# A hybrid decoder layer on one core: the sampled tokens' state space steps moved into tiles of their own, later, with a gate and a norm of their own, and the prompt's gate sums moved further behind their rows

## The chip, the cores and the metric

One core of a Trainium2 chip runs the whole kernel in one launch. The metric is the time of an execution on the device in microseconds (us); the figure for a kernel is the median of several runs. Engines are named as in the profile: PE (TensorE) does matmuls, DVE (VectorE), ACT (ScalarE) and POOL (GpSimd) do the elementwise work, SP issues transfers (DMA).

## The reference

One layer of a decoder on 1024 new prompt positions and 8 sampled tokens (one step each, with a past). Cut to what matters:

```
h = rmsnorm(x, norm1_w);  proj = h @ w_in          # columns: q, f, i, g, z, xBC, dt
o_a = HGRN2(q, f, i) ; o_a = rmsnorm(o_a) * silu(g)             # 8 heads of 128
xBC = silu(conv4(xBC));  X, B, C = split(xBC);  dt = softplus(dt + bias)
y = ssd_scan(X*dt, A*dt, B, C, S0) + D*X                        # 16 heads of 64, 2 groups
y = rmsnorm_per_group(y * silu(z)) * ssm_norm_w
x = x + concat(o_a, y) @ w_out
x = x + (silu(conv3(gate)) * val) @ w_down ;  out = rmsnorm(x)
```

For a sampled token `ssd_scan` is one step: new state S = exp(A dt) S0 + B (dt X), y = C S + D X. The prompt's 1024 positions are done in 8 chunks of 128. The kernel returns outputs and all the new states.

## The kernel before, in words

Activations lie with channels on the 128 partitions and tokens along the columns: NT = 1032 columns, the 1024 (T) of the prompt and behind them 8 (ND) of the sampled tokens. An input projection job (`in_job`, L290) makes 128 output channels: for each of 3 column chunks of 344 it issues 24 matmuls into one of three PSUM banks (`psmm`) and hands the bank to an eviction. 72 matmul steps make a job.

The order of PE's instructions is written by hand (`manual_schedule`, L1119). A list of jobs gives the backbone: x0 to x3, the B and C jobs and x4 to x7 (the conv'd channels of both state space groups), z0 to z3, the first head's f0, q0, v0, sg0, then z4 to z7, f1 and so on to head 7, then the output mix. `drive` (L266) steps through the jobs and puts the parts of another stream between their matmuls: the chunk steps of group 0 (`ssd(0)`, L713) run beside the jobs up to x7, those of group 1 from there up to v0, and each `head` in its turn. `after(n, work)` (L229) calls work n matmul steps later; what it issues on PE stands at that place. On the other engines a scheduler sets the order, and each engine keeps its queue.

A chunk step has two parts. `ssd_front` (L530) makes the decay matrix (csb: fetch, ACT Relu L541 and Exp L542, DVE L557), B C products (bg, bt), and transposed, scaled X (xp, xdt L554). `ssd_back` (L560) does the matmuls yo (with the state S), st and yd, the state update S (DVE L580) and the writing back into X's tile (L593).

The sampled tokens: `ssm_decode(g, i)` (L625) does one 128-channel tile. Twice, for 4 tokens each, it fetches Bb, Cb and the state Sd, scales Sd by the decay (4 ACT instructions, L638), multiplies Bb (DVE L639), adds (L640), stores the new state, multiplies by Cb (POOL L642) and reduces (DVE L643). Its result goes into columns 1024 to 1031 of the X tile. It is called at the beginning of jobs x5, x7, z0, z1 (group 0) and z4 to z7 (group 1).

`ssm_gate` (L653): each z job's eviction applies Silu (ACT L670), multiplies X's tile (DVE L671) and adds the squares to `gacc`. For the last z job of a group each chunk's sum goes to `rstd` (L681) 36 steps later in group 0, 50 in group 1: a matmul `ms` with ones sums over partitions, and `rstd_of` (L646) makes 1/sqrt on 344 columns (one ACT instruction from another function table and three DVE steps). After the last chunk `tail` (L690) scales the four X tiles of the group (DVE L694) and writes them to `mix_d` in DRAM, from where the output mix reads them after the heads.

Tiles come from pools (L42): "big" has 10 buffers of 1056 columns, so a head's q, v, sg and k wait for what lay there, X tiles among them. Matmul banks beside psmm's three: 4 "mx", 1 "nx" (ms, the head's vd and others).

A head's input (`head_in`, L806) evicts f, q, v and sg with Sigmoid, Silu, Copy and Silu (L818); f's end scales f (ACT L811) and makes k (DVE L812).

Of the kernel before, what the change touches and what calls it, by code (L numbers as in the profile page):

```python
# [8 lines left out]
F32 = mybir.dt.float32  # L9
F32R = mybir.dt.float32r  # L10
U8 = mybir.dt.uint8
AF = mybir.ActivationFunctionType
ALU = mybir.AluOpType
# [3 lines left out]
P = 128  # L17
DM = 1024
T = 1024
ND = 8  # L20
NT = T + ND
CH = 344
NCH = 3
# [27 lines left out]
def hybrid_layer(  # L51
# [9 lines left out]
    V, A, G, PE, SP = nc.vector, nc.scalar, nc.gpsimd, nc.tensor, nc.sync  # L61
# [9 lines left out]
    def nm(s):  # L71
        cnt[0] += 1
        return f"{s}_{cnt[0]}"
# [4 lines left out]
    const = part.enter_context(tc.tile_pool(name="const", bufs=1, side="right"))  # L78
    small = part.enter_context(tc.tile_pool(name="small", bufs=2, side="right"))
    tmp = part.enter_context(tc.tile_pool(name="tmp", bufs=1, side="right"))  # L80

    def tl(tag, name, dt=F32):
        w, n = TAGS[tag]
        return (work if tag in ("hT", "big", "e", "g") else tmp).tile([P, w], dt, tag=tag, bufs=n, name=nm(name))
# [4 lines left out]
    def bank(s, tag="mx"):  # L89
        return psmx.tile([P, 512], F32, tag=tag, bufs=NBANK[tag], name=nm(s))  # L90

    def mm(out, lhsT, rhs, start=True, stop=True):
        PE.matmul(out, lhsT, rhs, start=start, stop=stop)  # L93
# [55 lines left out]
    def col(name, i=0):  # L149
        c = vlay[name] + i  # L150
        return vcol[:, c:c + 1]
# [58 lines left out]
    chunks = [slice(c * CH, (c + 1) * CH) for c in range(NCH)]  # L210
# [18 lines left out]
    def after(n, work):  # L229

        later.append([n, work])
# [106 lines left out]
    Xg = [[None] * 4 for _ in range(2)]  # L338
    BT, CT, S = [None, None], [None, None], [None, None]
    last11 = const.tile([P, XT, 11], F32, name="last11")  # L340
    mix_d = dram.tile([16, P, NT], F32, name="mix_d")
    bc_d = dram.tile([4, ND, P], F32, name="bc_d")

    def conv_tail(acc, ext, nw, wname, bname, j, ntile, n):
        A.activation(acc[:, :n], ext[:, :n], AF.Identity, bias=col(bname, j), scale=col(wname, j))
        for q in range(1, nw):
            V.scalar_tensor_tensor(acc[:, :n], ext[:, q:q + n], col(wname, q * ntile + j), acc[:, :n],
                                   op0=ALU.mult, op1=ALU.add)

    def xbc_open():  # L350
        ext = tl("e", "ext")
        G.memset(ext[:, 0:3], 0.0)
        return ext

    def xbc_evict(j, ext, c, cs, ps):
        e = min(cs.stop, T)
        A.copy(ext[:, 3 + cs.start:3 + e], ps[:, :e - cs.start])
        if c == 2:
            V.tensor_copy(ext[:, 3 + T:3 + T + 32].rearrange("p (b r) -> p b r", r=4)[:, :, 3:4],
                          ps[:, T - cs.start:].unsqueeze(2))  # L360
            V.tensor_copy(last11[:, j, :], ps[:, CH - 11:])

    def xbc_close(j, ext):
        G.tensor_copy(ext[:, 3 + T:3 + T + 32].rearrange("p (b r) -> p b r", r=4)[:, :, 0:3],
                      bufT[:, j, :].rearrange("p (b r) -> p b r", r=3))
        n = T + 32
        acc = tl("big", "xbc")
        conv_tail(acc, ext, 4, "cw", "cb", j, XT, n)
        A.activation(acc[:, :T], acc[:, :T], AF.Silu)
        A.activation(acc[:, T:NT], acc[:, T + 3:T + 32:4], AF.Silu)  # L370
        return acc

    def xbc_job(j, put):
        ext = []
        def begin():
            ext.append(xbc_open())
            if j in (5, 7):
                ssm_decode(0, (5, 7).index(j))

        in_job(f"x{j}", OFF_X + j * P, lambda c, cs, ps: xbc_evict(j, ext[0], c, cs, ps), begin=begin, end=lambda: put(xbc_close(j, ext[0])))  # L380

# [20 lines left out]
    ones = keep.tile([P, P], F32, name="ones")  # L402
# [24 lines left out]
    for c, cs in enumerate(chunks):  # L427
        ps = psmm.tile([P, 512], F32, tag="mm", name=nm("dt"))
# [9 lines left out]
    for i in range(9):  # L438
        n = P if i < 8 else ND
# [171 lines left out]
    def d4(t):  # L611
        return t.rearrange("p (b n) -> p b n", n=P)
# [12 lines left out]
    def ssm_decode(g, i):  # L625
        j = g * 4 + i
        xdd = small.tile([P, 2, ND], F32, tag="xdd", name=nm("xdd"))
        xdec = Xg[g][i][:, T:NT]
        V.tensor_tensor(xdd[:, 0, :], xdec, ddb[:, 0, j, :], op=ALU.mult)
        for b0 in (0, 4):  # L630
            bs = slice(b0, b0 + 4)
            Bb, Cb = tl("d", "Bb")[:, :512], tl("d", "Cb")[:, :512]
            for t_, r in ((Bb, 2 * g), (Cb, 2 * g + 1)):
                fetch(t_, bc_d[r, bs].rearrange("b n -> (b n)").unsqueeze(0).to_broadcast([P, 512]))
            Sd = tl("ld", "Sd")
            fetch(d4(Sd), state_ssm[0, bs, 2 * j:2 * j + 2].rearrange("b h p n -> (h p) b n"))
            for b in range(4):
                A.activation(d4(Sd)[:, b, :], d4(Sd)[:, b, :], AF.Copy, scale=ddb[:, 1, j, b0 + b:b0 + b + 1])  # L638
            V.tensor_tensor(d4(Bb), d4(Bb), cb(xdd[:, 0, bs]), op=ALU.mult)  # L639
            V.tensor_tensor(Sd, Sd, Bb, op=ALU.add)  # L640
            SP.dma_start(ssm_sample[0, bs, 2 * j:2 * j + 2].rearrange("b h p n -> (h p) b n"), d4(Sd))
            G.tensor_tensor(Cb, Sd, Cb, op=ALU.mult)  # L642
            V.tensor_reduce(xdd[:, 1, bs], d4(Cb), axis=mybir.AxisListType.X, op=ALU.add)  # L643
        V.scalar_tensor_tensor(xdec, xdec, d_bc[:, j:j + 1], xdd[:, 1, :], op0=ALU.mult, op1=ALU.add)

    def rstd_of(dst, tmp, ps, n):  # L646

        A.activation(dst, ps, AF.Abs_reciprocal_sqrt, bias=epsc, scale=1.0 / n)
        V.scalar_tensor_tensor(tmp, ps, n * EPS, dst, op0=ALU.add, op1=ALU.mult)
        V.scalar_tensor_tensor(tmp, tmp, -0.5 / n, dst, op0=ALU.mult, op1=ALU.mult)  # L650
        V.scalar_tensor_tensor(dst, tmp, 1.5, dst, op0=ALU.add, op1=ALU.mult)

    def ssm_gate(g):  # L653
        acc = []

        def z_job(i):
            j = g * 4 + i

            def begin():
                if i == 0:  # L660
                    acc.append(tl("g", "gacc"))
                if g:
                    ssm_decode(1, i)
                elif i < 2:
                    ssm_decode(0, i + 2)

            def evict(c, cs, ps):
                Y = Xg[g][i][:, cs]
                sz = tl("z", "sz")[:, :CH]
                A.activation(sz, ps, AF.Silu)  # L670
                V.tensor_tensor(Y, Y, sz, op=ALU.mult)  # L671
                if i == 0:
                    A.activation(acc[0][:, cs], Y, AF.Square)
                else:
                    A.activation(sz, Y, AF.Square)
                    (V if g or i == 3 else G).tensor_tensor(acc[0][:, cs], acc[0][:, cs], sz, op=ALU.add)
                if i == 3:
                    after(36 + 14 * g, lambda: rstd(c))
            in_job(f"z{j}", OFF_Z + j * P, evict, begin=begin)

        def rstd(c):  # L681
            cs = chunks[c]
            ps = bank("ms", "nx")
            mm(ps[:, :CH], ones, acc[0][:, cs])
            rstd_of(acc[0][:, cs], tl("z", "nt")[:, :CH], ps[:, :CH], 512)

            if c == NCH - 1:
                tail()

        def tail():  # L690
            for i in range(4):
                j = g * 4 + i
                Y = Xg[g][i][:, :NT]
                V.scalar_tensor_tensor(Y, Y, col("sn", j), acc[0][:, :NT], op0=ALU.mult, op1=ALU.mult)  # L694
                SP.dma_start(mix_d[8 + j], Y)

        for i in range(4):
            z_job(i)
# [107 lines left out]
    def head_in(h):  # L806
        t = {}

        def f_end():
            f, k = t["f"], tl("big", "k")  # L810
            A.activation(f[:, :NT], f[:, :NT], AF.Identity, bias=lbt[:, 0, h:h + 1], scale=lbt[:, 1, h:h + 1])  # L811
            V.tensor_scalar(k[:, :NT], f[:, :NT], -1.0, 1.0, op0=ALU.mult, op1=ALU.add)  # L812
            t["k"] = k

        for n, off, func in (("f", OFF_F, AF.Sigmoid), ("q", OFF_Q, AF.Silu), ("v", OFF_I, AF.Copy),
                             ("sg", OFF_G, AF.Silu)):
            def evict(c, cs, ps, n=n, func=func):
                A.activation(t[n][:, cs], ps, func)  # L818

            def begin(n=n):  # L820
                t[n] = tl("e" if h == 0 and n == "f" else "big", n)

            if h == H - 1 and n == "sg":
                in_job_last(f"{n}{h}", off + h * P, evict, begin)
            else:
                in_job(f"{n}{h}", off + h * P, evict, begin, f_end if n == "f" else None)
        return t
# [539 lines left out]
    with tc.manual_schedule(engines={mybir.EngineType.PE}):  # L1367
# [56 lines left out]
        for r0 in range(0, FT - RND, RND):  # L1424
# [3 lines left out]
            for m in range(0, KT, 2):  # L1428
                wh, wl = wload(w_down[0, rows, m * P:(m + 2) * P], nk, 2 * P)
                for i in range(2):  # L1430
# [3 lines left out]
                    for c, cs in enumerate(quarters):  # L1434
                        ps = down(lambda k: (wh[:, k, :], wl[:, k, :]), nk, slice(i * P, (i + 1) * P), acts, c)
# [14 lines left out]
    for c in (3, 0, 1, 2):  # L1450
        cs = quarters[c]
        for m in range(KT):
            ps = down(lambda k: wd[k], nk, slice(m * P, (m + 1) * P), acts, c)
            V.tensor_tensor(xT[m][:, cs], xT[m][:, cs], ps, op=ALU.add)
        for t0 in range(cs.start, cs.stop, P):
            n = min(P, cs.stop - t0)
# [10 lines left out]
            for i in range(2):  # L1467
# [4 lines left out]
                else:  # L1472
                    V.scalar_tensor_tensor(ot[i][:n], tb[i][:n, :], ss[:n, 3:4], fw[:n, ds],  # L1473
                                           op0=ALU.mult, op1=ALU.mult)
# [31 lines left out]
```

## Time and profile before

| | |
|---|---|
| median of 3 runs | 1764.88 us (1764.72 to 1768.95) |
| the profiled execution | 1763.89 us, its span 1762.2 us |
| mean granted PE clock | 0.994 |
| PE busy in the span | 1713.2 us (97%) |
| DVE, ACT, POOL busy | 1105.4, 812.3, 482.0 us |

The profile is one execution. A line of the list of waits names the waiting engine and instruction, the instruction that released it, the total, the number and the longest of such waits. A line of the stretches gives for a window the busy time and number of instructions of each engine, the granted clock, the DMA share and GB/s. A line of a timeline starts with the start time and the duration; "x4" is four merged instructions, and what stands in brackets is idle time of the engine ahead of it and what ended it. L93 is the line of the helper that issues all matmuls.

### The profile page before, as it was taken

Reading aid. Unit: us, or ns where it says so; the run is one execution under the profiler, and the core shown is the slowest. Engines: PE = TensorE matmul, PEld = TensorE weight load, DVE = VectorE, ACT = ScalarE, POOL = GpSimd, SP = SyncE. Lnnn points to the kernel's source line nnn. Section 1 sums busy time; section 2 is a strip of 40 time slices with the busy share of each in tenths; the row PEclk is TensorE's granted clock in tenths of the full one; section 3 lists DMA queues with packets and bytes.
Section 4 is the critical chain, followed back from the end, with each engine's and each line's share of the span. In section 5 each row is a group of like instructions: output and inputs, shape, how many; then the busy total and the mean of one; then the engine's idle time right before and its main releaser. Section 6 shows DMA issues by size and latency. Waiting matters only on the chain. (4 is left out here: it accounts for less than half of the span.)

```text
span 1762.2 us, 38558 instructions
## 1 busy us (share of the span) xinstructions
PE 1713.2 (97%) x16111; PEld 1662.8 (94%) x16111; DVE 1105.4 (63%) x1988; ACT 812.3 (46%) x1450; POOL 482.0 (27%) x485
## 2 busy tenths in 40 slices
PE   7999899999999999999899999999999999999998
PEld 6999799998999999999799989999999999999997
DVE  6668966575554554466636688776667777445545
ACT  7577698454544454454423374334333434111114
POOL 2103332120110110112220355666666664000002
PEclk9999999999999999999899999999999999999999
DMA  5355744643321332234336742222222226422312
GB/s 166 68 147 155 189 117 136 179 139 105 88 89 51 98 87 80 69 115 143 110 113 212 245 127 73 73 85 85 85 73 73 80 78 217 152 85 78 98 61 97
DMA packets 249828, 199.17 MB, mean 113 GB/s; under 512 B 47212, under 2 KB 220822, under 8 KB 249638
## 3 DMA queue, kind: packets, MB, share of 16 engines
q1 hardware_dynamic: 249366, 196.61, 36.8%
q8 instruction: 126, 2.06, 0.5%
q14 instruction: 48, 0.39, 0.1%
q0 software_dynamic: 288, 0.10, 0.0%
HBM read 154.11 MB, written 46.94 MB: 114 GB/s over the span
## 5 line engine op out<-in xcount | busy, mean ns | idle before, releaser
L93 PE MATMUL mm<-hh,wh 128*128 128x344 f32 x1248 | 405.9, 326 | 2.0 <-issue 1.2
L93 PE MATMUL mm<-hl,wh 128*128 128x344 f32 x1248 | 405.5, 325 | 0.0
L93 PE MATMUL mm<-hh,wl 128*128 128x344 f32 x1248 | 402.4, 323 | 0.0
L93 PEld LDWEIGHTS mm<-hh,wh 128*128 128x128 f32 x1248 | 235.4, 189 | 6.5 <-issue 3.9
L93 PEld LDWEIGHTS mm<-hl,wh 128*128 128x128 f32 x1248 | 235.4, 189 | 4.5 <-issue 3.3
L93 PEld LDWEIGHTS mm<-hh,wl 128*128 128x128 f32 x1248 | 235.7, 189 | 1.8 <-issue 1.4
L190 ACT CAST wh<-ws 128x1024 fp32r<-128x1024 f32 x96 | 100.6, 1047 | 254.1 <-PE dn L93 135.0
L93 PE MATMUL ub<-uh,wh 128*128 128x258 f32 x704 | 199.3, 283 | 3.1 <-DVE fext L1319 2.7
L93 PE MATMUL ub<-ul,wh 128*128 128x258 f32 x704 | 199.0, 283 | 0.0
L93 PE MATMUL ub<-uh,wl 128*128 128x258 f32 x704 | 198.7, 282 | 0.0
L93 PE MATMUL dn<-ah,wh 128*128 128x256 f32 (+1 forms) x640 | 181.1, 283 | 2.0 <-DVE x L1436 2.0
L93 PE MATMUL dn<-al,wh 128*128 128x256 f32 (+1 forms) x640 | 180.6, 282 | 0.0
L93 PE MATMUL dn<-ah,wl 128*128 128x256 f32 (+1 forms) x640 | 180.1, 281 | 0.0
L192 DVE TENSOR_TENSOR wl<-ws,wh 128x1024 fp32r<-128x1024 f32 x88 | 108.7, 1235 | 75.7 <-ACT wh L190 68.6
L93 PE MATMUL mm<-mh,wh 128*128 128x258 f32 x512 | 148.2, 289 | 4.1 <-ACT x L1064 2.8
L93 PE MATMUL ua<-uh,wh 128*128 128x258 f32 x528 | 149.6, 283 | 1.3 <-DVE val L1331 1.3
L93 PE MATMUL ua<-ul,wh 128*128 128x258 f32 x528 | 149.3, 283 | 0.0
L93 PE MATMUL ua<-uh,wl 128*128 128x258 f32 x528 | 148.4, 281 | 0.0
L93 PE MATMUL mm<-ml,wh 128*128 128x258 f32 x512 | 146.9, 287 | 0.8 <-DVE ml L1024 0.8
L93 PE MATMUL mm<-mh,wl 128*128 128x258 f32 x512 | 146.5, 286 | 0.0
L93 PEld LDWEIGHTS ub<-uh,wh 128*128 128x128 f32 x704 | 132.9, 189 | 3.8 <-DVE fext L1319 2.9
L1269 DVE TENSOR_TENSOR wl<-wt,wh 128x512 fp32r<-128x512 f32 x88 | 89.6, 1037 | 74.2 <-ACT wh L1268 73.9
(351 smaller groups left out, 4037.2 us busy)
## 6 DMA issues: line engine op xcount, KB each, us to landing
ws<-in_w_in_dram SPq DMA_DIRECT2D x52, 512.0 KB
ws<-in_w_up_dram SPq DMA_DIRECT2D x44, 512.0 KB
ws<-in_w_out_dram SPq DMA_DIRECT2D x24, 512.0 KB
act_d<-val SPq DMA_DIRECT2D x22, 516.0 KB
al<-act_d SPq DMA_DIRECT2D x22, 516.0 KB
ws<-in_w_down_dram SPq DMA_DIRECT2D x22, 512.0 KB
ml<-mix_d SPq DMA_DIRECT2D x48, 172.0 KB
csb<-cs_d SPq DMA_DIRECT2D x32, 256.0 KB
```

The source lines that it names most:

```text
L93: PE.matmul(out, lhsT, rhs, start=start, stop=stop)
L190: A.copy(wh[:, :n], ws[:, :n])
L192: V.tensor_tensor(wl[:, :n], ws[:, :n], wh[:, :n].bitcast(F32), op=ALU.subtract)
L1269: V.tensor_tensor(lo[:, cs], sums[name], hi[:, cs].bitcast(F32), op=ALU.subtract)
```

## The change

The sampled tokens' columns get small tiles: `xdk` for X, later y, and `szd` for silu(z), both 128 x 8 x 8. `xbc_close` writes the decode columns of x0 to x7 into `xdk`; a z job's last eviction copies the decode columns of silu(z) into `szd` (POOL), and its other steps take the prompt's columns only. `ssm_decode` works on `xdk` and is called at other places: tile 0 at the beginning of z3, tiles 1 to 3 at f0, q0, v0, group 1's tile 0 at sg0, its tiles 1 to 3 at z4 to z6. A gate (`decode_gate`) comes 60 steps after the last decode of group 0, 180 after `tail` of group 1, and 40 steps later a norm with a matmul of its own (`decode_norm`), which writes one small piece to `mix_d` per group. `rstd` of both groups comes 100 steps after its rows, in place of 36 and 50; `tail` scales and writes 1024 columns.

```diff
+    xdk = const.tile([P, 8, ND], F32, name="xdk")
+    szd = const.tile([P, 8, ND], F32, name="szd")
...
-        A.activation(acc[:, T:NT], acc[:, T + 3:T + 32:4], AF.Silu)
+        A.activation(xdk[:, j, :] if j < 8 else acc[:, T:NT], acc[:, T + 3:T + 32:4], AF.Silu)
...
-            if j in (5, 7):
-                ssm_decode(0, (5, 7).index(j))
...
-        xdec = Xg[g][i][:, T:NT]
+        xdec = xdk[:, j, :]
...
+        if j == 3:
+            after(60, lambda: decode_gate(0))
+
+    def decode_gate(g):
+        js = slice(4 * g, 4 * g + 4)
+        dg = small.tile([P, 6, ND], F32, tag="dg", bufs=1, name=nm("dg"))
+        V.tensor_tensor(xdk[:, js, :], xdk[:, js, :], szd[:, js, :], op=ALU.mult)
+        V.tensor_tensor(dg[:, 0:4, :], xdk[:, js, :], xdk[:, js, :], op=ALU.mult)
+        V.tensor_reduce(dg[:, 4, :], dg[:, 0:4, :].rearrange("p j b -> p b j"), axis=mybir.AxisListType.X, op=ALU.add)
+        after(40, lambda: decode_norm(g, js, dg))
+
+    def decode_norm(g, js, dg):
+        ps = bank("dgs", "nx")
+        mm(ps[:, :ND], ones, dg[:, 4, :])
+        rstd_of(dg[:, 4, :], dg[:, 5, :], ps[:, :ND], 512)
+        for j in range(js.start, js.stop):
+            V.scalar_tensor_tensor(xdk[:, j, :], xdk[:, j, :], col("sn", j), dg[:, 4, :], op0=ALU.mult, op1=ALU.mult)
+        SP.dma_start(mix_d[8 + js.start:8 + js.stop, :, T:NT].rearrange("j p b -> p j b"), xdk[:, js, :])
...
-                if g:
-                    ssm_decode(1, i)
-                elif i < 2:
-                    ssm_decode(0, i + 2)
+                if g and i < 3:
+                    ssm_decode(1, i + 1)
+                elif j == 3:
+                    ssm_decode(0, 0)
...
             def evict(c, cs, ps):
+                cs = slice(cs.start, min(cs.stop, T))
+                n = cs.stop - cs.start
...
+                if c == NCH - 1:
+                    G.tensor_copy(szd[:, j, :], sz[:, n:])
+                sz = sz[:, :n]
...
-                    after(36 + 14 * g, lambda: rstd(c))
+                    after(100, lambda: rstd(c))
...
-                Y = Xg[g][i][:, :NT]
-                V.scalar_tensor_tensor(Y, Y, col("sn", j), acc[0][:, :NT], op0=ALU.mult, op1=ALU.mult)
-                SP.dma_start(mix_d[8 + j], Y)
+                Y = Xg[g][i][:, :T]
+                V.scalar_tensor_tensor(Y, Y, col("sn", j), acc[0][:, :T], op0=ALU.mult, op1=ALU.mult)
+                SP.dma_start(mix_d[8 + j][:, :T], Y)
+            if g:
+                after(180, lambda: decode_gate(1))
...
             def begin(n=n):
+                if h == 0:
+                    i = "fqvs".index(n[0])
+                    ssm_decode(*((0, i + 1) if i < 3 else (1, 0)))
```

`rstd` takes the same limits on its columns as `evict`.

More of the change, by code (lines that the diff above doesn't have):

```diff
@@ L677, in evict @@
                 if i == 3:
-                    after(36 + 14 * g, lambda: rstd(c))
+                    after(100, lambda: rstd(c))
             in_job(f"z{j}", OFF_Z + j * P, evict, begin=begin)
         def rstd(c):
-            cs = chunks[c]
+            cs = slice(chunks[c].start, min(chunks[c].stop, T))
+            n = cs.stop - cs.start
             ps = bank("ms", "nx")
-            mm(ps[:, :CH], ones, acc[0][:, cs])
-            rstd_of(acc[0][:, cs], tl("z", "nt")[:, :CH], ps[:, :CH], 512)
+            mm(ps[:, :n], ones, acc[0][:, cs])
+            rstd_of(acc[0][:, cs], tl("z", "nt")[:, :n], ps[:, :n], 512)
             if c == NCH - 1:
```

## The prediction

> **What bounds the kernel now.** I read the page first, then the list of what TensorE waited for, then the busy time by stretches of the part that the change touches (150 to 450 us), then the single instructions around the longest waits. From the page, the busy times:
>
> ```profile
> PE 1713.2 (97%) x16111; PEld 1662.8 (94%) x16111; DVE 1105.4 (63%) x1988; ACT 812.3 (46%) x1450; POOL 482.0 (27%) x485
> ```
>
> TensorE is the bound: 49 us of 1762 without work. So a moved instruction of another engine is worth only the TensorE waits that it makes or ends. The waits that lie in the change's reach, from the list of TensorE's waits (total, times, longest):
>
> ```profile
> PE yo L93 <- DVE S L580: 3.1, 1, 3.1
> PE a L93 <- DVE q L873: 2.8, 1, 2.8
> PE mm L93 <- ACT x L1064: 2.8, 1, 2.8
> PE ms L93 <- DVE vd L842: 1.4, 1, 1.4
> PE yd L93 <- DVE xdt L554: 1.4, 2, 1.0
> PE a L93 <- DVE v L873: 0.7, 2, 0.5
> PE xp L552 <- DVE S L580: 0.6, 2, 0.4
> ```
>
> yo, yd and xp wait at 176 to 205 us, in the chunk steps of the first state space group (jobs x5 to x7); ms and a at 383 to 411 us, around job z7 and the first head. The row for mm<-x is at 839 us, outside, and is here for comparison. Busy time by stretches (sums of TensorE, its loads, DVE, ACT, POOL, then the granted clock, the DMA share and GB/s):
>
> ```profile
> 150.00:200.00 50.00, 48.06 (x339) 43.65 (x339) 45.66 (x75) 38.58 (x84) 18.42 (x17) 1.00 0.73 188
> 200.00:250.00 50.00, 46.86 (x315) 43.04 (x314) 37.63 (x66) 37.02 (x73) 15.17 (x11) 0.97 0.56 147
> 250.00:300.00 50.00, 49.74 (x348) 45.13 (x346) 38.62 (x68) 45.12 (x80) 11.44 (x10) 1.00 0.39 121
> 300.00:350.00 50.00, 50.00 (x338) 47.98 (x335) 26.77 (x49) 22.36 (x48) 10.47 (x9) 1.00 0.61 179
> 400.00:450.00 50.00, 46.72 (x553) 45.07 (x542) 25.57 (x47) 24.04 (x37) 0.00 (x0) 0.97 0.29 90
> ```
>
> With DVE at 45.66 of 50 us the chunk steps stall; with DVE at 38.62 (250 to 300) the same steps of the second group run almost without a gap (49.74), though ACT is then at 45.12. From 300 on both have room.
>
> **Part 1: two decodes leave x5 to x7 (gain).** The groups of DVE instructions from 150 to 206 us, those of the decode:
>
> ```profile
> L640 DVE TENSOR_TENSOR Sd<-Sd,Bb 128x512 f32<-128x512 f32 x4 | 3.7, 916 | 0.0
> L643 DVE TENSOR_REDUCE xdd<-Cb 128x4 f32<-128x512 f32 x5 | 3.4, 680 | 3.4 <-POOL Cb L642 3.4
> L639 DVE TENSOR_TENSOR Bb<-Bb,xdd 128x512 f32<-128x512 f32 x4 | 3.2, 801 | 1.9 <-DMA Bb<-bc_d 1.9
> ```
>
> That is 10.3 us of busy time, and 5.3 us in which DVE stood idle until their inputs came, with the chunk steps queued behind. Without them DVE falls from 45.66 to about 37 in this stretch, below the 38.62 at which the second group shows next to no gap. So I let all of it go: yo 3.1 + yd 1.4 + xp 0.6 = 5.1 us. The clock comes with it:
>
> ```profile
> 204.00:214.00 10.00, 9.06 (x56) 7.44 (x57) 10.00 (x23) 3.77 (x10) 2.35 (x2) 0.83 0.58 141
> 404.00:414.00 10.00, 6.72 (x155) 6.35 (x155) 9.40 (x14) 4.26 (x7) 0.00 (x0) 0.85 0.70 256
> 836.00:844.00 8.00, 3.06 (x139) 2.61 (x139) 8.00 (x11) 3.92 (x9) 4.86 (x4) 1.00 0.87 242
> ```
>
> After the 3.1 us wait the ten us ran at 0.83, so 1.7 us more were lost; after the 2.8 us wait at 409 us at 0.85, 1.5 us. **Part 1: -6.8 us** (bounds: -8 with small gaps that go unseen, -2 if only the small waits go).
>
> The third row shows another 2.8 us wait (mm for x) behind which the clock stayed at 1.00, so the loss is not certain.
>
> The Trainium skill ("TensorE: Matmul & The Clock Gate", What's actually happening) puts the fall to half clock behind an idle window of about 3.4 us. By that, the waits of 2.8 and 3.1 us would have cost no clock; the rows at 0.83 and 0.85 speak against it, the one at 1.00 for it. What it would make of the time is the fourth rival below.
>
> **Part 2: gate sums of group 0 later, and three decodes in z3, f0, q0 (loss).** In the changed order the ms matmuls of group 0 go from behind chunk 2 of z3 and within f0 into f0 and q0; the last stands as the second matmul of q0's chunk 1. Behind it come rsqrt (ACT), three DVE steps, tail's scaling and the writes to mix_d. q0's tile takes the place of x0's in the ten buffers of "big", so q0's first eviction waits for x0's mix write. v0's first matmul needs the bank that this eviction empties (three banks). In before the tail ran during q0 chunks 0 and 1, ahead of it. What decides is ACT's queue in order, so I add it up from the chunk step within f0's chunk 0 to q0's first eviction. The durations, from ACT's timeline (start, us):
>
> ```profile
> 286.59 0.55 ACT L648 ACTIVATE gacc<-ms,epsc 128x344 f32<-128x344 f32 x1
> 287.15 1.28 ACT L818 ACT_TABLE_LOAD   x1
> ...
> 290.48 1.04 ACT L190 CAST wh<-ws 128x1024 fp32r<-128x1024 f32 x1
> 291.42 0.44 ACT L818 ACTIVATE f<-mm 128x344 f32<-128x344 f32 x1
> ...
> 293.17 0.64 ACT L542 ACTIVATE csb<-csb 128x512 f32<-128x512 f32 x1
> 293.71 1.24 ACT L811 ACTIVATE f<-f,lbt 128x1032 f32<-128x1032 f32 x1
> 294.86 1.26 ACT L541 ACTIVATE csb<-csb,cst 128x128 f32<-128x128 f32 x4
> 296.02 0.25 ACT L548 COPY bt<-bg 128x128 f32<-128x128 f32 x1
> 296.17 0.63 ACT L542 ACTIVATE csb<-csb 128x512 f32<-128x512 f32 x1
> 296.82 1.28 ACT L818 ACT_TABLE_LOAD   x1
> 298.12 0.46 ACT L818 ACTIVATE q<-mm 128x344 f32<-128x344 f32 x1
> 301.06 0.46 ACT L818 ACTIVATE q<-mm 128x344 f32<-128x344 f32 x1 [2.49 <-PE mm L93]
> ```
>
> Starts are closer than durations, so I use steps between starts: four csb scalings 294.86 to 296.02, 0.29 each; bt 0.15; a table load 1.30; cast 0.94; the 1032-column f 1.15; exp 0.60; rsqrt 0.56; an eviction 0.46. The changed order holds in that stretch 24 csb scalings and 14 Sd scalings of the decode (same 128x128 shape; before had none there): 38 x 0.29 = 11.0; 11 table loads 14.3; 6 exp 3.6; 3 rsqrt 1.7; 3 f evictions 1.4; 2 casts 1.9; f 1.15; 3 bt 0.45; one square 0.5. Sum 36.0, with q's own eviction 36.5 us. TensorE's time for the same stretch lies between these two rows of its timeline, with the group of the ms matmuls from 250 to 312 us behind them:
>
> ```profile
> 273.33 0.42 PE L93 MATMUL mm<-hh,wl 128*128 128x344 f32 x1
> 305.34 0.40 PE L93 MATMUL mm<-hh,wh 128*128 128x344 f32 x1
> ```
>
> ```profile
> L93 PE MATMUL ms<-gacc,ones 128*128 128x344 f32 x6 | 2.4, 486 | 0.3 <-DVE nt L649 0.3
> ```
>
> The second is v0's first matmul. 305.3 - 273.3 = 32.0, with one ms more (2.4 / 6 = 0.4 each) and without the 0.3 us wait there 32.1. So v0 starts 36.5 - 32.1 = 4.4 us late, of which I keep 4.3, and since that is longer than 3.1 us the half clock costs about 1.6 more. The mix write itself is not last. Between the last rsqrt of ms and q's eviction ACT still has 14 scalings (4.1), two loads (2.6), two exp (1.2), a cast (0.9) and a bt: 9.0 us. Against that stand three DVE steps and one scaling of tail, under 3 us, and a transfer. The same wait in before, of q1's eviction for mix_d (ACT's timeline), and tail's scalings on DVE:
>
> ```profile
> 405.73 1.28 ACT L818 ACT_TABLE_LOAD   x1 [2.12 <-DMA mix_d<-xbc]
> ```
>
> ```profile
> 401.65 4.90 DVE L694 SCALAR_TENSOR_TENSOR xbc<-xbc,vcol,gacc 128x1032 f32<-128x1032 f32 x4
> 406.47 0.69 DVE L812 TENSOR_SCALAR k<-f 128x1032 f32<-128x1032 f32 x1
> ```
>
> The first scaling ended a quarter of 4.90 behind 401.65, at 402.9, and the load started at 405.7: 2.8 us for the transfer, in all under 6. **Part 2: +5.9 us.** Lower end 0: ACT's queue reaches q's eviction in time if its steps pack tighter. Upper end: ACT idled 4.3 us for csb transfers between 250 and 312 us in before:
>
> ```profile
> ACT csb L541 <- DMA csb<-cs_d: 4.3, 5, 2.1
> ```
>
> If that stays, the wait is 8.6 us and two half-clock windows 3.4: +12.0. I take 4.3, since an ACT that is behind finds its csb rows landed.
>
> The Trainium skill ("ScalarE: Activation LUTs", What ACT_TABLE_LOAD costs) gives about 2.66 us for a switch of the table, a drain of 1.38 us included. By that, eleven switches would put an estimated 15 us more on ACT's sum and the time near 1773 us. The rows show none of it (rsqrt ends at 287.14, the load starts at 287.15, takes 1.28 us, and the next instruction starts 0.02 us behind such a load), so it gets no chance of its own.
>
> **Part 3: z7 to the first head (gain).** In before tail(1), the 4.9 us from 401.65, stands on DVE ahead of the first head's k and scalings, and the "a" matmuls waited 2.8 + 0.5 us for those. With 100 steps of delay DVE has those scalings ahead of tail(1), whose results nothing on TensorE needs before the output mix behind the heads. The one bank of ms was held by the head's vd (1.4 us); the ms comes later and finds it free. So 1.4 + 2.8 + 0.5 + 1.5 (clock) = 6.2 us go. Against it, q1's eviction now waits for the mix write of x4, by the same count of queue steps about level with what v1 needs; I set 0.5 us. **Part 3: -5.7 us** (bounds -6.2 and, if q1's wait is like q0's, 0).
>
> **Part 4: the rest.** Two added dgs matmuls of 8 columns, +0.3 us (at most 0.8, by ms's 0.4 for 344 columns); two rsqrt with table loads, where ACT has 22 to 24 us of 50; gate and norm on DVE, 32 columns at most, where it has 26 to 27; POOL's copies of 8 columns, with POOL at 18 of 50 or less; one small DMA per group and four shorter ones on SP, behind which loads wait that are due a job later. If that cover is gone, some 3 us (two loads of 1.28). Group 1's decodes come one job earlier (sg0, z4 to z6), into the stretch with DVE 26.77 and ACT 22.36.
>
> **Sum** on the profiled execution, 1763.89 us with a span of 1762.2 (0.06% under the median of 1764.88): -6.8 + 5.9 - 5.7 + 0.3 = -6.3, so **1757.6 us**, 0.4% under the median.
>
> **The rivals.**
> - *Part 2's wait is hidden* (ACT packs tighter): -12.2, 1751.7 us. For it: in before ACT waited 2.49 us for TensorE ahead of q's second eviction (row 301.06). Against: it now has 14 x 0.29 = 4.1 us of Sd scalings more there. 0.10.
> - *ACT's idle time stays as well*: +12.0 in place of 5.9, so 1763.7 us, no change. 0.18. That the change's gains don't come (S still late because the conv of x7 holds DVE) gives about the same, 1764 us: 0.10.
> - *The second group becomes what the first was* (slower). Three decodes, 10.3 / 2 = 5.1 us of DVE each, enter 250 to 300 us: 38.62 + 15.4, less the 4.9 of tail that leaves, 49.1 us of 50, more than the 45.66 at which the first group stalled for 5.1 us. From about 45 of 50 on, S of one chunk step is late for yo of the next. Scaled by three decodes to two that is 7.7, with two half-clock windows 11.1, on top of part 2: 1757.6 + 11.1 = 1768.7, with part 2 at 8.6 us of wait 1774. Against it: POOL is emptier there (11.44 against 18.42 us), DVE's large conv steps are over, and part of the third decode falls behind 300 us. 0.15.
> - *The clock is not given back* (the 0.83 and 0.85 have another cause than the waits, as the 1.00 behind 2.8 us suggests): parts 1 and 3 lose 3.2 and part 2 keeps its 1.6, so 1760.8 us. 0.10.
>
> **Chances.** Forecast 0.37, its own range 1754 to 1760. About 0.3% (5.3 us) is what a measurement can tell from no change; the bounds are then 1759.6 and 1770.2. Faster: the forecast, the hidden wait and a little of the fourth rival, 0.50. Same: second and third rivals, most of the fourth, the lower end of the slower one, 0.38. Slower 0.12. The range 1751 to 1769 leaves out the upper half of the slower case and a little below.
>
> **What would show it.** Right: no wait of yo for S at 190 to 205 us and a clock of 1.00 there; a wait of 3 to 6 us of v0's first matmul, for ACT's q, at about 300 us, with ACT busy 48 or more of the 50 us ahead of it; no wait of a for q, and of ms for vd, near 400 us. Wrong: gaps of yo or yd between 250 and 300 us (the slower rival), a gap of over 7 us at v0, or waits in sg0 to z6, where I expect none.

## The result, and the profile after

The changed kernel takes 1770.82 us (median of 20 runs, 1766.35 to 1777.02) where before takes 1765.11 (20 runs, 1761.58 to 1770.98): 0.27% slower, ratio 1.0027, interval 1.0020 to 1.0035. The forecast was 1757.6, its range ended at 1769, and the sign was wrong. The profiled execution of the changed kernel took 1774.53 us, 3.7 above its median.

What TensorE waited for between 240 and 340 us, changed kernel:

```profile
PE mm L93 <- ACT q L845: 5.2, 1, 5.2
PE ms L93 <- DVE nt L668: 5.2, 2, 2.9
PE sT L606 <- DVE S L581: 1.7, 1, 1.7
PE xp L553 <- DVE ecs L575: 0.7, 1, 0.7
PE yd L93 <- DVE xdt L555: 0.4, 1, 0.4
```

In before the same stretch had one wait of 0.3 us. The stretches of the changed kernel (columns as ahead of the prediction's; the clock is the third number from the end):

```profile
150.00:200.00 50.00, 50.00 (x357) 46.20 (x358) 41.03 (x68) 34.49 (x70) 14.26 (x13) 1.00 0.49 124
250.00:300.00 50.00, 43.69 (x278) 39.16 (x277) 37.43 (x68) 45.57 (x85) 17.56 (x16) 0.93 0.62 174
204.00:214.00 10.00, 10.00 (x67) 9.96 (x66) 7.32 (x11) 9.61 (x17) 0.00 (x0) 1.00 0.52 160
285.00:325.00 40.00, 32.36 (x188) 29.29 (x189) 29.72 (x57) 25.39 (x52) 13.48 (x8) 0.87 0.63 190
416.00:426.00 10.00, 9.30 (x204) 8.54 (x204) 8.62 (x11) 3.71 (x7) 0.00 (x0) 1.00 0.53 211
```

The old gaps are closed: 50.00 of 50 from 150 to 200 (48.06 before), a clock of 1.00 at 204 to 214 (0.83) and behind the first head's start (0.85). A new hole is open at 285 to 325: PE 32.36 of 40 at a clock of 0.87.

To see where time goes I compare the start of each job's first matmul in the two timelines, for instance z3 and sg0 in before and in the changed kernel:

```profile
253.97 0.31 PE L93 MATMUL mm<-hh,wh 128*128 128x344 f32 x1
...
323.07 0.41 PE L93 MATMUL mm<-hh,wh 128*128 128x344 f32 x1
```

```profile
246.79 0.31 PE L93 MATMUL mm<-hh,wh 128*128 128x344 f32 x1
...
334.20 0.40 PE L93 MATMUL mm<-hh,wh 128*128 128x344 f32 x1
```

At z3 the changed kernel is 7.2 us ahead, at sg0 11.1 us behind: 18.3 us lost between. In the same way: x5 to z0 wins 7.5; z6 to v1 wins 5.9 (from 12.4 behind to 6.6); the following head's dg matmul and small things lose 1.1; at the start of the up projection it is 7.6 behind. The rest of the profiled execution's 10.6 us is mostly a wait of 2.5 us there, for x (L1096); it differs from profile to profile (none in before, 0.5 us in e1, 1.9 in e2) and I do not count it to the change.

### The profile page after: what moved, and what is told of

The parts are those of the page before. It is cut to its first block, busy times and chain, and to the rows that moved or that the text cites. A ratio compares the mean times of both kernels' runs of the same rounds, so it can differ in the third digit from the quotient of the medians.

```text
span 1772.8 us, 38615 instructions
## 1 busy us (share of the span) xinstructions
PE 1719.1 (97%) x16115; PEld 1668.6 (94%) x16115; DVE 1107.6 (62%) x2008; ACT 813.3 (46%) x1453; POOL 487.6 (28%) x493
```

## The experiments

Each run's median, beside before on the same chip, and in the last column the loss from z3's to sg0's first matmul against before (from the profiles, as above):

| run | gate sums of group 0 | decodes of group 0 | q0's buffer | median us | ratio to before, interval | z3 to sg0 |
|---|---|---|---|---|---|---|
| changed | 100 | z3, f0, q0, v0 | x0's | 1770.82 | 1.0027 (1.0020 to 1.0035) | +18.3 |
| e1 | 36 | z3, f0, q0, v0 | x0's | 1762.32 | 0.998 (0.997 to 0.999) | +6.7 |
| e2 (before, 100) | 100 | x5, x7, z0, z1 | x0's | 1768.79 | 1.0016 (1.0006 to 1.0025) | +7.0 |
| e3 | 100 | sg0, z4 to z6 | x0's | 1783.6 | 1.0107 (1.0092 to 1.0122) | +9.5 |
| e4 | 36 | sg0, z4 to z6 | x0's | 1775.37 | 1.0051 (1.0038 to 1.0064) | +2.1 |
| e5 | 100 | z3, f0, q0, v0 | own | 1765.74 | 0.9999 (0.9987 to 1.0011) | +8.2 |
| e6 (ms in other banks) | 100 | z3, f0, q0, v0 | x0's | 1770.96 | 1.0034 (1.0021 to 1.0047) | +16.2 |
| e7 | 36 | z1, f0, q0, v0 | x0's | 1765.92 | 1.0013 (1.0003 to 1.0022) | +6.3 |
| e8 (e7, group 1 at 50) | 36 | z1, f0, q0, v0 | x0's | 1765.41 | 1.0001 (0.9991 to 1.0010) | +6.1 |
| e9 | 36 | z0, z1, v0, sg0 | x0's | 1764.22 | 0.9996 (0.9984 to 1.0007) | +4.8 |
| e10 | 100 | z0, z1, v0, sg0 | own | 1767.61 | 1.0013 (1.0001 to 1.0025) | +3.9 |
| e11 | 36 | f0, q0, v0, sg0 | x0's | 1761.76 | 0.998 (0.9968 to 0.9991) | +2.0 |
| e12 (no Sd scaling) | 100 | z3, f0, q0, v0 | x0's | 1774.6 | 1.0058 (1.0039 to 1.0076) | +21.2 |
| e13 | 100 | f0, q0, v0, sg0 | own | 1766.1 | 1.0015 (1.0003 to 1.0028) | +8.1 |
| e14 | 100 | f0, q0, v0, sg0 | x0's | 1771.15 | 1.0032 (1.0016 to 1.0048) | +13.1 |

**The two halves apart: e1 to e4.** Theory A: the late gate sums cost the time. Theory B, the rival: the decodes in z3 to q0 do, by load. e1's edit:

```diff
-                    after(100, lambda: rstd(c))
+                    after(100 if g else 36, lambda: rstd(c))
```

> The changed kernel with the gate sums of group 0 36 steps behind their rows again, as before; decodes, tiles and group 1's 100 steps stay. Theory A (the late gate sums cost the time: with one bank for ms each ms matmul waits for the reading of the one ahead in a late ACT queue, and q0's eviction is queued behind tail's mix write): no waits of ms over 1 us and none of v0 for q between 260 and 320 us; the 18.7 us lost from f0 to sg0 shrink to under 5, time 1754 to 1758 us. Theory B (the decodes in z3 to q0 cost it, by ACT and DVE load, wherever the gate sums stand): 10 us or more stay lost there, time 1764 to 1770 us.

e2's, on the kernel before:

```diff
-                    after(36 + 14 * g, lambda: rstd(c))
+                    after(50 if g else 100, lambda: rstd(c))
```

> The kernel before with one number changed: group 0's gate sums 100 steps behind their rows in place of 36; decodes at x5, x7, z0, z1 as before, no small tiles. Theory A: waits of ms and of v0 for q appear at 280 to 315 us, 12 to 18 us with the clock, time 1775 to 1783 us. Theory B: under 3 us are lost there, time 1764 to 1768 us. In both the waits at 176 to 205 us stay.

e3's (e4 has e1's edit too):

```diff
-                if g and i < 3:
-                    ssm_decode(1, i + 1)
-                elif j == 3:
-                    ssm_decode(0, 0)
+                if g:
+                    ssm_decode(*((0, i + 1) if i < 3 else (1, 0)))
...
-                if h == 0:
-                    i = "fqvs".index(n[0])
-                    ssm_decode(*((0, i + 1) if i < 3 else (1, 0)))
+                i = "fqvs".index(n[0])
+                if h == 0 and i == 3:
+                    ssm_decode(0, 0)
+                elif h == 1 and i < 3:
+                    ssm_decode(1, i + 1)
```

> The changed kernel with all decodes later: group 0's at sg0, z4, z5, z6, group 1's at z7, f1, q1, v1; gate sums at 100 steps stay. Theory A: ms and v0 still wait, 8 us or more from f0 to sg0 in place of 18.7, time 1760 to 1768 us. Theory B: f0 to sg0 loses under 4 us, time 1751 to 1757 us.

> Both: group 0's gate sums at 36 steps and all decodes late. By either theory nothing is left to lose from f0 to sg0 and the gains at x5 to x7 (7 us) and z7 to the first head (5 us) stay: 1751 to 1756 us. If the decodes in z7 to v1 cost the first heads something, 1757 to 1762 us.

e1 wins 8.5 us on the changed kernel; v0 no longer waits. But it missed theory A's 1754 to 1758, because one wait stayed, in z3. TensorE's waits from 240 to 340 us in e1, in e2 and in e3:

```profile
PE ms L93 <- DVE gacc L700: 3.5, 1, 3.5
...
```

```profile
PE mm L93 <- ACT q L818: 4.0, 1, 4.0
...
```

```profile
PE mm L93 <- ACT q L843: 5.2, 1, 5.2
...
PE ms L93 <- DVE nt L668: 0.8, 1, 0.8
```

v0's wait for q is there without any decode from z2 to v0 (e2, e3): it belongs to the late sums alone. The long ms waits are not there without those decodes. In the last column late sums cost 11.6 beside the decodes (18.3 - 6.7) and 7.4 without (9.5 - 2.1); the decodes cost 8.8 and 4.6. Both theories hold a part, A the larger; neither holds alone. e2's median misses theory A's 1775, though its 7.0 us of loss is clear; e3 and e4 as totals missed every expectation, since the decodes put late cost TensorE elsewhere. TensorE's waits in e4, 340 to 480 us:

```profile
PE ms L93 <- DVE nt L668: 5.2, 1, 5.2
PE a L93 <- DVE v L931: 4.6, 1, 4.6
...
```

So the jobs beside the first head (z7, f1, q1, v1) are no free place either.

**What holds v0 and ms: e5, e6.**

```diff
-                t[n] = tl("e" if h == 0 and n == "f" else "big", n)
+                t[n] = tl("e" if h == 0 and n in "fq" else "big", n)
```

> The changed kernel with q0's tile in the free second buffer of the tag that f0 uses, so that its eviction no longer waits for x0's mix write; gate sums at 100 steps and all decodes stay. If the buffer behind tail is what makes v0 wait (5.2 us in the changed kernel): no wait of v0 for q over 1 us, the ms waits of 2.9 and 2.3 us stay, 5 to 7 us are won, 1763 to 1766 us. If a full ACT queue makes it (the sum of the prediction): v0 or the next evictions still wait 3 us or more, under 3 us are won, 1768 to 1771 us.

```diff
-            ps = bank("ms", "nx")
+            ps = bank("ms", "nx" if g else "mx")
```

> The changed kernel with group 0's ms matmuls in the four rotating banks in place of the single one. If the single bank is what stops TensorE at ms: the waits of 2.9 and 2.3 us go, and with them one or two half-clock windows; v0's wait for q stays or grows by part of them, since ACT stays as late; 2 to 7 us are won, 1764 to 1769 us. If the rotating banks are held up as long: the waits come back as waits of bg, yo or st, nothing is won, 1769 to 1773 us.

TensorE's waits from 240 to 340 us, e5 and then e6:

```profile
PE ms L93 <- DVE nt L668: 5.2, 2, 2.9
...
```

```profile
PE mm L93 <- ACT q L845: 5.0, 1, 5.0
PE yd L93 <- DVE ecs L575: 3.0, 1, 3.0
...
PE yo L93 <- DVE xdt L555: 1.1, 1, 1.1
PE st L93 <- DVE nt L668: 0.7, 1, 0.7
...
```

The buffer in e5 takes v0's wait away and 5.1 us off the median. q's first eviction now stands much earlier in ACT's order, ahead of the next csb work (ACT's timeline of e5; in the changed kernel all three q evictions stand at 312.64):

```profile
298.77 0.46 ACT L845 ACTIVATE q<-mm 128x344 f32<-128x344 f32 x1
```

e6 takes the ms waits away and gets 4.8 us of yo, st and yd waits for them: the single bank is only where lateness shows. Nothing is won.

**Is it ACT's scaling load: e12.** This is the prediction's own sum put to the test; without the scalings the sampled tokens' new state and y lack the decay.

```diff
-            for b in range(4):
-                A.activation(d4(Sd)[:, b, :], d4(Sd)[:, b, :], AF.Copy, scale=ddb[:, 1, j, b0 + b:b0 + b + 1])
```

> The changed kernel without ACT's eight scalings of the sampled state in each decode, so the new state and y of the sampled tokens leave out the decay. It takes 2.4 us of ACT a decode away, everything else stays. If ACT's Sd scalings make v0 late (the sum of the prediction, 14 of them, 4.1 us): v0's wait for q falls from 5.2 to about 1 us. If the place of q's eviction in ACT's order does it, behind tail and the next csb: v0 still waits 4 us or more. The ms waits (2.9 and 2.3 us) go if ACT's lateness by these scalings makes them, and stay if DVE's and POOL's part of the decode does. 1762 to 1766 us if only the ms waits go, under 1760 if both.

TensorE's waits in e12 from 240 to 340 us, then ACT's from 250 to 316:

```profile
PE mm L93 <- ACT q L843: 4.7, 1, 4.7
PE ms L93 <- DVE nt L666: 3.0, 1, 3.0
PE xp L553 <- DVE ecs L575: 2.9, 1, 2.9
...
```

```profile
ACT sz L697 <- DVE xbc L693: 10.3, 4, 3.3
...
```

With every scaling gone v0 waits 4.7 us against 5.2, and the time is no better (1774.6). ACT now stands idle 10.3 us for DVE's gate product (of z2's last chunk and of z3's three), with DVE's part of the decode ahead of it: what TensorE loses is not set by ACT's scalings alone. The other engines' order changes too when they are left out, so e12 does not price them.

**Where can the decodes stand: e7, e9, e10, e11.** e7, e9 and e11 have e1's edit too (36 steps), e10 has e5's (the buffer) and 100 steps. e7's edit:

```diff
-                elif j == 3:
+                elif j == 1:
                     ssm_decode(0, 0)
```

> Group 0's gate sums at 36 steps and decode tile 0 of group 0 at the beginning of z1 in place of z3; all else as changed. If in the run with 36 steps the 3.5 us wait of ms (with two half-clock windows, 6.0 us from z3 to f0) came from decode tile 0 ahead of the gate sums in DVE's queue, it goes: 1755 to 1758 us. If it comes from something else, it stays: 1760 to 1764 us.

e9 and e10 call decodes of group 0 at z0, z1, v0, sg0 and of group 1 at z4 to z7:

```diff
-                if g and i < 3:
-                    ssm_decode(1, i + 1)
-                elif j == 3:
-                    ssm_decode(0, 0)
+                if g:
+                    ssm_decode(1, i)
+                elif i < 2:
+                    ssm_decode(0, i)
...
-                if h == 0:
-                    i = "fqvs".index(n[0])
-                    ssm_decode(*((0, i + 1) if i < 3 else (1, 0)))
+                if h == 0 and n in ("v", "sg"):
+                    ssm_decode(0, 2 + (n == "sg"))
```

> Small tiles kept; group 0's gate sums at 36 steps, group 1's at 100; decodes of group 0 at z0, z1, v0, sg0, so that none stands in z2 to q0, those of group 1 at z4 to z7 as before. Theory now: TensorE's waits at ms come from ACT and DVE being late by the decodes in z3 to q0, v0's wait from q0's buffer behind a late tail. With neither, f0 to sg0 loses under 2 us, the 7 us at x5 to x7 stay won, and z7 to the first head keeps 2 to 5: 1755 to 1759 us. Rival: the decodes' work is only pushed about and shows up as new waits of 5 us or more at z0 to z3 or v0 to z7: 1762 to 1767 us.

> The same places of the decodes, with both groups' gate sums at 100 steps as in the changed kernel and q0's tile in a buffer of its own. Theory now: with the buffer apart and no decode in z2 to q0 the 100 steps of group 0 cost nothing: no wait of ms or v0 over 1 us, within 2 us of its twin with 36 steps, 1755 to 1760 us. Rival: late gate sums in f0 and q0 stop TensorE by themselves: 5 us or more above the twin.

e11 leaves out the `elif i < 2` of e9 and calls `ssm_decode(0, "fqvs".index(n[0]))` for h == 0:

> Small tiles kept, group 0's gate sums at 36 steps, group 1's at 100, decodes of group 0 at f0, q0, v0, sg0 and of group 1 at z4 to z7. In the run with 36 steps and the decodes of the change one wait was left, 3.5 us of ms in z3 with 6.0 us in all, where DVE had decode tile 0 ahead of the gate sums. If that decode's place is the cause, the wait goes and 4 to 6 us are won on that run, 1756 to 1759 us. If the decode only brings the same wait to where it now stands (f0 or later, or z7 to the first head), the time stays at 1761 to 1766 us.

e7 missed: the 3.5 us ms wait of z3 goes, a 2.7 us one comes in f0. e9 missed too, and its rival was right; its waits from 185 to 340 us:

```profile
PE sT L606 <- DVE xdk L645: 3.5, 1, 3.5
PE sT L606 <- DVE S L581: 2.5, 1, 2.5
...
```

The decodes' work now meets the end of each state space group (the transposes sT of S): DVE had decode steps ahead of the last S there, and 4.3 of the 7.5 us won from x5 to z0 are lost again. e10 missed its forecast (no ms wait over 1 us, 1755 to 1760) and lies 3.4 us above its twin e9, under the 5 that its rival named. The sT waits are there too, and a ms wait of 2.5 us (1.5 in e9). Whether the late sums cost anything here is not shown: the intervals overlap, and from z3 to sg0 e10 loses less than e9. TensorE's waits in e10, 185 to 340 us:

```profile
PE sT L606 <- DVE S L581: 4.8, 2, 3.1
PE ms L93 <- DVE nt L668: 2.5, 1, 2.5
...
```

e11 is best with e1: 0.2% faster than before, with 2.0 us lost from z3 to sg0. It then loses 5.1 us to late z evictions (340 to 480 us), so it ends above the 1756 to 1759 I expected if that wait went:

```profile
PE mm L93 <- ACT sz L689: 5.1, 4, 2.2
...
```

**Buffer and late sums with no decode in z3: e13, e14.** Both are e11 with 100 steps for group 0; e13 has e5's buffer too.

> The best places of the decodes (group 0 at f0 to sg0, group 1 at z4 to z7), both groups' gate sums at 100 steps, q0's tile in a buffer of its own. If decode tile 0 in z3 and q0's buffer behind tail are the whole cause: no ms wait over 1.5 us, v0 does not wait, 1760 to 1763 us, as its twin with 36 steps (1761.8). If late gate sums in f0 and q0 stop TensorE by themselves: ms waits of 2 us or more stay and the time is 1764 to 1768 us.

> The same with q0's tile back in x0's buffer. If the buffer costs v0's wait whatever stands beside it: 4 to 6 us of wait at v0, with the clock 5 to 8 us above the run with the buffer apart. If it needed the decode in z3 too: under 2 us of wait, the same time.

Waits from 240 to 340 us, e13 and then e14:

```profile
PE ms L93 <- DVE nt L668: 5.4, 1, 5.4
...
```

```profile
PE ms L93 <- DVE nt L668: 5.4, 1, 5.4
PE mm L93 <- ACT q L843: 4.4, 1, 4.4
```

36 steps 1761.8, 100 steps with a buffer apart 1766.1, with x0's buffer 1771.2: by the medians the late sums by themselves cost 4.3 us and the buffer 5.0, about as in e5. The intervals of e11 and e13 stand apart, those of e13 and e14 overlap; there the wait of v0 (none, and 4.4 us) decides. My thought behind e13, that decode tile 0 and the buffer were the whole cause, fell: the ms wait is 5.4 us without that decode.

**Group 1's 100 steps: e8**, e7 with `after(50 if g else 36, ...)`.

> The same with group 1's gate sums at 50 steps as before. If the 100 steps of group 1 took away the waits of ms for vd and of a for q at 384 to 411 us (part 3 of the prediction), these come back here: 3 to 6 us slower than its twin with 100 steps, 1759 to 1763 us. If it was the decodes that left z7 (group 1's come one job earlier in both), both have the same time within 1 us.

TensorE's waits from 375 to 430 us in e8, and then in e7:

```profile
PE a L93 <- DVE q L903: 2.6, 1, 2.6
PE a L93 <- DVE v L903: 0.5, 1, 0.5
```

```profile
PE mm L93 <- ACT q L845: 1.2, 1, 1.2
```

The a waits come back at 50 steps, so the delay is what took them away; the wait of ms for vd does not come back, so its going is not shown to be the delay's work. From z7's to v1's first matmul e7 wins 3.7 us and e8 1.9. The medians (1765.92, 1765.41) lie within 1 us, as the other branch of the expectation had it, and do not show that difference.

## Why the prediction was wrong

**What bounds it** held: TensorE, and all that changed were its waits.

**Part 1 was right.** -6.8 forecast; -7.5 in the profile, waits and clock both gone. Only the load was misjudged: DVE is busy 41.03 of 50 us from 150 to 200 where I had about 37, and TensorE has no gap all the same.

**Part 2 failed**: +5.9 forecast, +18.3 in the profile. The step that failed is the sum of ACT's queue set against TensorE's time, with v0 as the only wait. Three things in it:

- *The ms waits, 5.2 us, were not in the sum at all.* I counted what ACT had to do up to q's eviction, and for TensorE only what it issues. The order that I had read has each later ms waiting for DVE's reading of the one before, and that waits for ACT's rsqrt. ACT's timeline of the changed kernel:

```profile
272.06 0.40 ACT L639 ACTIVATE Sd<-Sd,ddb 128x128 f32<-128x128 f32 x1
...
282.30 0.46 ACT L845 ACTIVATE f<-mm 128x344 f32<-128x344 f32 x1
282.77 1.28 ACT L667 ACT_TABLE_LOAD   x1
284.07 0.55 ACT L667 ACTIVATE gacc<-ms,epsc 128x344 f32<-128x344 f32 x1
...
304.15 1.28 ACT L542 ACTIVATE csb<-csb,cst 128x128 f32<-128x128 f32 x4 [4.25 <-DMA csb<-cs_d]
...
311.35 1.28 ACT L845 ACT_TABLE_LOAD   x1
312.64 1.16 ACT L845 ACTIVATE q<-mm 128x344 f32<-128x344 f32 x3
```

  The first ms was issued at 275 us; its rsqrt starts at 284.07, behind two f evictions and their table loads, and the second ms, due at 282.3, waits 2.9 us to 285.2.

- *v0's wait was right in place and size (4.3 forecast, 5.2 measured), but not for the reason given.* ACT did not carry a backlog into it: it stood idle 4.25 us ahead of 304.15. SP's timeline of the changed kernel shows why:

```profile
300.76 0.32 SPq L175 DMA_DIRECT2D csb<-cs_d  x1
...
306.82 4.51 SPq L720 DMA_DIRECT2D mix_d<-xbc  x4
```

  The csb fetch goes out only when TensorE's yo is through (300.7), and q's eviction, which must wait for tail's write (306.8), stands behind all of that csb work in ACT's order. Three q chunks, two of them long computed, leave in one piece at 312.64. From yo it is a chain of 12 us, whatever ACT did before; removing the scalings (e12) leaves it, a buffer apart (e5, e13) ends it. The write itself is not last: at the 2.8 us that such a transfer took in before, it would have landed at an estimated 309.6, some 3 us ahead of q's eviction.

  The sum of ACT's work was good. From 272.06, where ACT begins the work that I had added up, to q's eviction at 312.64 are 40.6 us, 4.25 of them idle: 36.3 us of work where I had 36.0. What failed stands beside it. I let ACT begin level with TensorE, and it begins 6.0 us behind the matmul from which I counted (273.33 in before; the first row below). Before's own rows had it some 2.9 us behind at this place (the csb step that starts at 276.21). I set the idle time to nothing, "since an ACT that is behind finds its csb rows landed", and it was 4.25: this is the "ACT's idle time stays" rival, to which I gave 0.18. And TensorE, which I gave 32.1 us for the stretch, took 47.1, since it lost time at ms, to the clock and at v0:

```profile
266.04 0.42 PE L93 MATMUL mm<-hh,wl 128*128 128x344 f32 x1
...
313.15 0.66 PE L93 MATMUL mm<-hh,wh 128*128 128x344 f32 x1 [5.18 <-ACT q L845]
```

  So v0 starts 15.0 us later than those 32.1 us would have it, where I had 4.4; the 6.0 and the 4.25 make up nearly all of the difference. That about 5 of the 15.0 show as v0's own wait, near my 4.3, is chance.
- *The clock.* 40 us at 0.87 are 5.2 us, where I had 1.6 for one window. With sT's 1.7 (S late behind the late v0), xp and yd the parts add up: 5.2 + 5.2 + 1.7 + 1.1 + 5.2 = 18.4.

**Part 3** was right in size: -5.7 forecast, -5.9 from z6 to v1; no a wait, ms 0.7, q 0.7 (0.5 forecast). e8 shows the delay as the cause of the a waits, though no median shows it, and not as the cause of the ms wait's going.

**Part 4**: +0.3 forecast, about +1.1, half of it a wait of 0.5 us for dg.

**The rivals.** The slower one (waits of yo and yd like the first group's) did not occur: 0.4 us of yd, 0.7 of xp. That its times (1768.7 and 1774) lie around the measured 1770.8 is chance. What it reads from DVE's share was wrong: 37.43 of 50, less than the 38.62 of before, since DVE was held up rather than full. The 0.83 and 0.85 did go with the waits, so the fourth rival fell. The row that spoke for it ended too early: the window with the 2.8 us wait for x stops at 844 us with 1.00, and right behind it the clock fell there too (before; another wait, of 1.9 us, lies between):

```profile
844.00:848.00 4.00, 4.00 (x22) 4.00 (x22) 4.00 (x8) 2.36 (x6) 0.00 (x0) 0.57 0.95 275
```

So -7.5 + 18.3 - 5.9 + 1.1, with some 1.6 ahead of x5 and between sg0 and z6, is +7.6 in the profile; the medians differ by 5.7.

**Open:** how the 5.4 us of ms wait divides among ACT's evictions, table loads and DVE in e13; no run takes these apart. Why the decodes in z3 to q0 and the late sums together cost 4.2 us more in the profiles than singly is not shown; in the medians, the changed kernel and e14 (no decode in z3) do not differ.

## What to carry to other kernels

A result that is moved later keeps its buffer longer, and whoever takes that buffer over is late with it: look up which tile comes next in the ring before you delay the last reader, and count on the scheduler putting the waiting eviction behind other work on its engine. A sum over one engine's queue is no forecast of a chain that goes TensorE, transfer, ACT, DVE and back; follow each matmul that waits back to what it issues itself. The best versions (e1, e11, 0.2% faster than before) keep the part that opened a full stretch, the decodes out of x5 to x7, and leave group 0's sums where they were.

## What the runs showed of the hardware

The clock does not follow the length of a wait. Waits of TensorE of nearly one length: of e2 and of e10 the instruction that waited (its timeline row) and the ten us around and behind it, of e1 the ten us of its 3.5 us wait of ms (above, at 264 us), of e9 those of its 3.5 us wait of sT (above, at 324 us):

```profile
208.92 2.05 PE L93 MATMUL yo<-xbc,S 128*128 128x128 f32 x8 [3.12 <-DVE S L580]
```

```profile
208.00:218.00 10.00, 9.08 (x50) 7.21 (x51) 9.67 (x22) 3.27 (x10) 2.35 (x2) 0.67 0.54 141
```

```profile
209.02 0.66 PE L606 MATMUL sT<-ident,S 128*128 128x128 f32 x4 [3.15 <-DVE S L581]
```

```profile
209.00:219.00 10.00, 9.98 (x65) 9.94 (x66) 10.00 (x16) 8.27 (x17) 1.33 (x1) 1.00 0.44 129
```

```profile
263.00:273.00 10.00, 9.11 (x48) 7.71 (x49) 9.07 (x17) 7.66 (x13) 2.70 (x2) 0.69 0.53 161
324.00:334.00 10.00, 9.43 (x61) 9.46 (x62) 8.38 (x18) 6.06 (x13) 2.58 (x2) 1.00 0.73 211
```

Behind a wait of 3.12 us the ten us ran at 0.67 of the clock, which is 3.3 us lost (before's own 3.1 us wait at this place cost 1.7), and behind one of 3.5 us at 0.69; other waits of 3.15 and 3.5 us cost nothing. The Trainium skill ("TensorE: Matmul & The Clock Gate", What's actually happening) has the gate watch a free-running window, which fits that the same wait costs differently from run to run. By its idle window of about 3.4 us the wait of 3.12 could not have filled one and should have been free, and its row says otherwise; a wait of 3.5 fills one only where it happens to lie right, so those two rows don't speak against it. A wait of about 3 us is therefore worth anything from 3 to 6.4 us.
